# A SwiGLU block on one core: where the sums of activations are split into high and low parts, and by which engine

## The chip, the cores and the metric

The kernel runs on one core of a Trainium2 chip. The metric is the device time of one execution, in microseconds. The core has a matrix engine (TensorE, PE in the profile), three engines for elementwise work (VectorE as DVE, ScalarE as ACT, GpSimd as POOL), and SyncE (SP), which here issues most of the DMA transfers. Each engine carries out its own instructions in order; between engines there are semaphores only. SBUF is the on-chip memory from which the engines work, PSUM the banks that TensorE accumulates into.

## The reference

One decoder block: a SwiGLU feed-forward network, a mixer of three branches (RWKV-7, sparse attention, cross-attention to a memory), and a second SwiGLU network. The change touches the two SwiGLU networks alone, each of which computes, with S = 1024 tokens, D_MODEL = 1024 and D_FF = 2816:

```python
def _rmsnorm(x, g):
    xf = x.astype(jnp.float32)
    y = xf * lax.rsqrt(jnp.mean(xf * xf, axis=-1, keepdims=True) + NORM_EPS)
    return (y * g.astype(jnp.float32)).astype(x.dtype)

def _swiglu(h, w_gate, w_up, w_down):
    return (jax.nn.silu(h @ w_gate) * (h @ w_up)) @ w_down
...
x = x + 0.5 * _swiglu(_rmsnorm(x, ffn1_norm[l]), ffn1_w_gate[l], ffn1_w_up[l], ffn1_w_down[l])
...
x = x + 0.5 * _swiglu(_rmsnorm(x, ffn2_norm[l]), ffn2_w_gate[l], ffn2_w_up[l], ffn2_w_down[l])
return _rmsnorm(x, final_norm)
```

All in float32.

## The kernel before

**Numbers in two parts.** Every operand of a product is split into a high part in the type fp32r and a low part, the rest: `split` (L100 to L106) makes the high part by a copy on ACT (L103) and the low part by a subtraction on DVE or POOL (L106). `mm3` (L121 to L125) then issues three matmuls for each 128x128 block of weights: high by high (L123), high weights by low activations (L124), low weights by high activations (L125). Names in the profile: `whi` and `wlo` are the parts of weights, `wraw` weights as loaded (by SP, L110), `wS` and `ds` sums of weights, `h` and `t` the moving operands of the gates, `act` those of the down product, `rg` a tile of the ring described below.

**Gates.** The class `Gates` computes gate and up products and from them the activations. D_FF has 22 columns of 128 (f = 0 to 21). Columns 0, 1, 20 and 21 (`PLAIN`) keep their activations as they are; the other eighteen make nine pairs. In `run`, products are not computed as four blocks of a 2x2 scheme but as seven (Winograd's form): P1, P2, P6, P5, P7, P3, P4, the names of `ORDER`. One product of a pair's gate or up side is 12 matmuls of 128x128 by 128x512 that accumulate in a PSUM bank; P6 adds to P1's bank and P7 adds to P6's, so before P7 may add, an ACT copy has to take P6's value out of the bank (`copy`, L502, into a ring tile). P6, P5 and P7 follow each other.

**The sums.** `finish` gets each finished up product, multiplies it with the gate's (L387) and stores the activation to DRAM (`ad`). When the four activations a11, a12, a21, a22 of a pair are there, it forms the four sums that the down product, also in Winograd's form, needs: P5 (L401), P7 (L402), P6 (L403) and P4 (L404), one POOL subtraction after another, each into a tile of a ring of `RING` = 10 tiles. Each sum is split on the spot: a high part by ACT (L409), a low part by DVE (L410). Both parts are stored, eight stores of 256 KB per pair (L413).

**Tail.** `tail` is the down product. Its 18 middle columns go in three thirds (c = 0, 1, 2); each third has 28 products: seven groups (the names of `ORDER`) for four column pairs dp of the output, in two halves of 14 (dp 0 and 1, then 2 and 3). One product is 9 matmuls. A group is three activations of the same name; `load(g)` (L254 to L266) brings them in: the sums P5, P7, P6 and P4 come already split, by two DMAs each straight into the operand tiles (L262); the other groups come raw into one of three buffers `ar` (L265) and are split by L266, for the second of three with the low part on POOL, otherwise on DVE. The first two groups are loaded and split by `first`, while the gates end. Groups 2 to 7 are loaded as the tail begins, each later one during the second half of a third (`if dp == 3`). The weights' parts are prepared `AHEAD` = 3 products ahead. The results are added to x by DVE from PSUM (L287) or by an ACT copy to `dc` (L291) and a POOL addition (L293). Sixteen products of 12 matmuls for the plain columns end the tail.

**What sets the order.** A scheduler of the framework reorders the instructions of the program before each engine's queue is written, so an engine's order is not that of the source; the printed rows in the section on the change are from the written queues. Tiles of one tag share a fixed number of buffers, and a new tile waits for the last reader of the one whose buffer it takes.

Of the kernel before, what the change touches and what calls it, by code (L numbers as in the profile page):

```python
# [8 lines left out]
FT = mybir.dt.float32  # L9
FR = mybir.dt.float32r  # L10
AF = mybir.ActivationFunctionType
# [8 lines left out]
HALF = 512  # L20
ORDER = "P1", "P2", "P6", "P5", "P7", "P3", "P4"
PLAIN = 0, 1, 20, 21
SUMS = "P5", "P7", "P6", "P4"
NG = 8
RING = 10
AHEAD = 3
# [6 lines left out]
class Builder:  # L33
# [203 lines left out]
    def tail(self, x, wd, ad, act, xload, after, st=None):  # L237
# [3 lines left out]
        nc = self.nc  # L241
# [3 lines left out]
        pool = st.enter_context(self.tc.tile_pool(name="ffd", bufs=1, space=PSUM, reuse_waits="tile"))  # L245
# [8 lines left out]
        def load(g):  # L254

            for j, src in enumerate(groups[3 * g:3 * g + 3]):
                n = (g % NG) * 6 + 2 * j
                t = [slots[n + p][0].tile([128, HALF], FR, name=f"act{g}{j}{p}", tag=slots[n + p][1]) for p in range(2)]
                act.append(t)
                if isinstance(src, list):  # L260
                    for a, b in zip(t, src):
                        nc.sync.dma_start(a.bitcast(FT), b)  # L262
                    continue
                raw = temp("ar", HALF, 3)
                nc.sync.dma_start(raw, src)  # L265
                self.split(*t, raw, eng_lo="pool" if j == 1 else "dve")  # L266

        def blocks(c, dp):

# [34 lines left out]
        xload(0)  # L304
        xload(2)
        load(2)
        xload(1)
        xload(3)
        for g in range(3, NG):
            load(g)  # L310
        for n, (c, dp, i, g) in enumerate(ops):
# [3 lines left out]
            name = ORDER[i]  # L315
            b = banks.setdefault((c, dp), {})
# [24 lines left out]
            if dp == 3 and 3 * (g + NG) < len(groups):  # L341
                load(g + NG)
# [11 lines left out]
class Gates:  # L354
# [15 lines left out]
    def temp(self):  # L370
        return self.p.tile([128, HALF], FT, name="wS", tag="wS", bufs=3)

    def finish(self, f, half, gu, c, r=None):

        nc = self.nc
        if gu == 0:
            if r is not None:
                g = self.ring()
                nc.vector.tensor_mul(g, c, r)
                c = g  # L380
            th = self.ring()
            nc.scalar.activation(th, c, AF.Tanh, scale=0.5)
            sg = self.sg[f, half] = self.p.tile([128, HALF], FT, name="sg", tag="sg", bufs=SG)
            nc.vector.scalar_tensor_tensor(sg, th, 1.0, c, op0=OP.add, op1=OP.mult)
            return
        sg = self.sg.pop((f, half))
        nc.vector.tensor_mul(sg, sg, c)  # L387
        if r is not None:
            nc.vector.tensor_mul(sg, sg, r)
        if f in PLAIN:  # L390
            (nc.scalar if f >= 20 else nc.sync).dma_start(self.ad[f, half], sg)
            return
        pair, n = f // 2, f % 2 * 2 + half
        q = self.act.setdefault(pair, {})
        q[n] = sg
        if n != 1:
            nc.sync.dma_start(self.ad[pair, ("P1", None, "P2", "P3")[n]], sg)
        if len(q) == 4:
            a11, a12, a21, a22 = [q[j] for j in range(4)]
            t = {j: self.ring() for j in ("P5", "P7", "P6", "P4")}  # L400
            nc.gpsimd.tensor_sub(t["P5"], a12, a11)  # L401
            nc.gpsimd.tensor_sub(t["P7"], a22, a12)  # L402
            nc.gpsimd.tensor_sub(t["P6"], a22, t["P5"])  # L403
            nc.gpsimd.tensor_sub(t["P4"], a21, t["P6"])  # L404
            parts = {}
            for j in t:
                hi = self.ring().bitcast(FR)
                parts[j] = hi, t[j].bitcast(FR)
                nc.scalar.activation(hi, t[j], AF.Copy)  # L409
                nc.vector.tensor_sub(parts[j][1], t[j], hi.bitcast(FT))  # L410
            for j in t:
                for a, b in zip(self.ad[pair, j], parts[j]):
                    nc.sync.dma_start(a, b.bitcast(FT))  # L413
            del self.act[pair]

    def plain(self, fs, halves, h, r=None, loads=None, step=None):
# [973 lines left out]
class Mem:  # L1390
# [76 lines left out]
    def attend(self, m, p, po):  # L1467
# [15 lines left out]
        for j in range(4):  # L1483
# [26 lines left out]
            if late:  # L1510
                finish(*late.pop())
            late.append((j, ph, pl))
            yield
        yield
        finish(*late.pop())
        yield

# [21 lines left out]
def body(ctx, tc, A, VO):  # L1539
    nc = tc.nc  # L1540
    B = Builder(ctx, tc, A)
    drp = ctx.enter_context(tc.tile_pool(name="spill", bufs=1, space=DRAM))
# [28 lines left out]
    ad = {(f, i): drp.tile([128, HALF], FT, name=f"ah{f}{i}") for f in PLAIN for i in range(2)}  # L1571
    for p in range(1, 10):
        for n in ORDER:
            t = [drp.tile([128, HALF], FT, name=f"ad{p}{n}{j}") for j in range(2 if n in SUMS else 1)]
            ad[p, n] = t if n in SUMS else t[0]
    x2d = [drp.tile([128, S], FT, name=f"x2d{k}") for k in range(KT)]
    xnd = [drp.tile([128, HALF], FT, name=f"xnd{k}") for k in range(KT)]
    xs, ns = ExitStack(), ExitStack()
# [11 lines left out]
    with ExitStack() as fs:  # L1590
# [47 lines left out]
        with ExitStack() as st:  # L1638
            B.tail(x, A["wd1"], ad, act, lambda k: nc.sync.dma_start(x[k], A["xT"][k]),
                   finish(x, np_, nps, into(x, np_, VO["mix_norm"], h),  # L1640
                          lambda half, d: nc.sync.dma_start(x1d[d][:, halves[half]], x[d][:, halves[half]])),
                   st)
# [126 lines left out]
    with ExitStack() as fs:  # L1769
        np_, nps = B.norm_pool(fs)  # L1770
        B.more_w(fs)
        with ExitStack() as st:
# [31 lines left out]
            with tc.tile_pool(name="mgp", bufs=1, reuse_waits="tile") as mp, \  # L1804
                    tc.tile_pool(name="mgps", bufs=1, space=PSUM, reuse_waits="tile") as mps:
                raw = lambda tag: mp.tile([128, HALF], FT, name=tag, tag=tag, bufs=3)
# [122 lines left out]
```

## Time and profile before

| | us |
|---|---|
| Median of three runs | 3010.19 |
| Lowest and highest | 3002.58, 3011.4 |
| The profiled execution | 3008.93 |
| Its span | 3007.1 |

The stages of the profiled execution, cut at round moments near their borders, each with the matmuls recorded in it:

| Stage | from to (us) | length (us) | matmuls |
|---|---|---|---|
| Start and plain columns | 0 to 131 | 131.0 | 425 |
| Gates, first network (`run`) | 131 to 518.4 | 387.4 | 1495 |
| Tail, first network, and the step to the mixer | 518.4 to 763 | 244.6 | 1002 |
| Mixer | 763 to 2140 | 1377.0 | 7231 |
| Its end, and the second network's plain columns | 2140 to 2380 | 240.0 | 988 |
| Gates, second network | 2380 to 2764 | 384.0 | 1495 |
| Tail, second network | 2764 to 2990 | 226.0 | 946 |
| Final norm | 2990 to 3007 | 17.0 | 2 |

In a row of the profile that names a group, the first field is the line of the kernel, then the engine, the operation, and the tiles as output<-inputs with their sizes; behind the bar come busy time and mean length in ns, and then the time that the engine stood idle just before these instructions, with the engine and line that released it. In a row of the timeline the first two numbers are the start and the length in us, and brackets hold the idle time before it. The granted clock is the share of full speed that TensorE was allowed in that stretch.

### The profile page before, as it was taken

How to read it: one execution, taken by the hardware profiler on the slowest of the kernel's cores; microseconds unless marked ns; L12 is line 12 of the kernel's file. 1: busy time of each engine (PE TensorE's matmuls, PEld its weight loads, DVE VectorE, ACT ScalarE, POOL GpSimd, SP SyncE). 2: the span in 40 equal slices, each digit the busy share in tenths (PEclk: the TensorE clock that was granted, in tenths of full speed). 3: DMA queues.
4: the chain of work that ended last, by engine and by line, in shares of the span. 5: the costliest groups of instructions: out<-in, count | busy, mean ns of one | idle time of the engine just before them, and what ended most of it. 6: DMA issues, size and time to landing. Idle time of an engine off the chain costs nothing. (4 is left out here: it accounts for less than half of the span.)

```text
span 3007.1 us, 40911 instructions
## 1 busy us (share of the span) xinstructions
PE 2837.3 (94%) x13574; PEld 2241.2 (75%) x13574; DVE 1935.4 (64%) x3876; ACT 1373.5 (46%) x2923; POOL 1012.6 (34%) x981
## 2 busy tenths in 40 slices
PE   7899999999999999999999989999999999999997
PEld 5777777787887677776777667777787777777786
DVE  8656555767565567666565357888767466565676
ACT  5334434444454345444453356666544333334343
POOL 4434343674102011111110133333324343344672
PEclk9999999999999999999999999999999999999998
DMA  4333435754313122221222552221564333336653
GB/s 151 99 117 129 143 130 171 274 178 150 117 57 91 56 71 64 75 72 56 68 65 64 157 164 74 80 70 60 179 219 141 96 127 105 121 119 221 230 176 98
DMA packets 241520, 363.70 MB, mean 121 GB/s; under 512 B 50291, under 2 KB 90107, under 8 KB 241308
## 3 DMA queue, kind: packets, MB, share of 16 engines
q1 hardware_dynamic: 223696, 330.38, 33.8%
q10 hardware_dynamic: 17612, 30.70, 3.4%
q8 instruction: 107, 1.75, 0.2%
q14 instruction: 105, 0.86, 0.1%
HBM read 257.59 MB, written 103.40 MB: 120 GB/s over the span
## 5 line engine op out<-in xcount | busy, mean ns | idle before, releaser
L103 ACT ACTIVATE whi<-wraw 128x512 fp32r<-128x512 f32 (+1 forms) x584 | 353.2, 607 | 701.8 <-PE pgu L124 309.6
L106 DVE TENSOR_TENSOR wlo<-wraw,whi 128x512 fp32r<-128x512 f32 (+1 forms) x576 | 454.7, 794 | 303.8 <-ACT whi L103 284.7
L123 PE MATMUL mm<-h,whi 128*128 128x512 f32 x800 | 329.9, 412 | 0.2 <-ACT gbt L1662 0.2
L125 PE MATMUL mm<-h,wlo 128*128 128x512 f32 x800 | 320.8, 402 | 7.2 <-DVE wlo L106 7.2
L124 PE MATMUL mm<-h,whi 128*128 128x512 f32 x800 | 318.6, 398 | 0.0
L123 PE MATMUL pgu<-t,whi 128*128 128x512 f32 x576 | 238.0, 413 | 57.7 <-ACT rg L502 57.7
L123 PE MATMUL pgu<-h,whi 128*128 128x512 f32 x688 | 273.6, 398 | 16.8 <-ACT whi L103 15.9
L125 PE MATMUL pgu<-h,wlo 128*128 128x512 f32 x688 | 273.9, 399 | 8.0 <-DVE wlo L106 7.9
L124 PE MATMUL pgu<-h,whi 128*128 128x512 f32 x688 | 275.2, 400 | 2.2 <-DVE h L98 1.7
L123 PE MATMUL pd<-act,whi 128*128 128x512 f32 x632 | 248.7, 393 | 7.4 <-ACT whi L103 7.4
L125 PE MATMUL pd<-act,wlo 128*128 128x512 f32 x632 | 248.5, 393 | 4.5 <-DVE wlo L106 4.3
L124 PE MATMUL pd<-act,whi 128*128 128x512 f32 x632 | 247.9, 392 | 0.0
L125 PE MATMUL pgu<-t,wlo 128*128 128x512 f32 x576 | 235.4, 409 | 0.0
L124 PE MATMUL pgu<-t,whi 128*128 128x512 f32 x576 | 234.9, 408 | 0.0
L123 PEld LDWEIGHTS pgu<-t,whi 128*128 128x128 f32 x576 | 114.3, 198 | 90.5 <-ACT rg L502 66.6
L125 PEld LDWEIGHTS mm<-h,wlo 128*128 128x128 f32 x800 | 151.5, 189 | 39.9 <-DVE wlo L106 9.0
L123 PEld LDWEIGHTS mm<-h,whi 128*128 128x128 f32 x800 | 151.8, 190 | 36.4 <-issue 5.3
L124 PEld LDWEIGHTS mm<-h,whi 128*128 128x128 f32 x800 | 151.9, 190 | 28.8 <-issue 3.0
L123 PEld LDWEIGHTS pgu<-h,whi 128*128 128x128 f32 x688 | 132.8, 193 | 47.3 <-ACT whi L103 18.9
L125 PEld LDWEIGHTS pgu<-h,wlo 128*128 128x128 f32 x688 | 132.9, 193 | 40.3 <-DVE wlo L106 11.9
L124 PEld LDWEIGHTS pgu<-h,whi 128*128 128x128 f32 x688 | 133.1, 193 | 32.6 <-DVE h L98 2.7
L123 PEld LDWEIGHTS pd<-act,whi 128*128 128x128 f32 x632 | 119.8, 190 | 34.2 <-ACT whi L103 9.5
(419 smaller groups left out, 6615.6 us busy)
## 6 DMA issues: line engine op xcount, KB each, us to landing
wraw<-in_wgu SPq DMA_DIRECT2D x192, 256.0 KB, 2.7
wraw<-in_wd SPq DMA_DIRECT2D x96, 192.0 KB, 4.2
wraw<-in_win SPq DMA_DIRECT2D x52, 256.0 KB, 2.6
wraw<-in_wgb SPq DMA_DIRECT2D x48, 256.0 KB, 2.8
gd<-gbt SPq DMA_DIRECT2D x48, 256.0 KB, 2.0
gbt<-gd ACTq DMA_DIRECT2D x40, 256.0 KB, 2.9
wraw<-in_wd SPq DMA_DIRECT2D x32, 256.0 KB, 2.7
wraw<-in_wbr SPq DMA_DIRECT2D x32, 256.0 KB, 3.1
```

Source lines behind the costliest of these rows:

```text
L103: nc.scalar.activation(hi, src, AF.Copy)
L106: (nc.vector if eng_lo == "dve" else nc.gpsimd).tensor_sub(lo, src, hi.bitcast(FT))
L123: mm(ps, w[0], x[0], start=start, stop=False, **kw)
L124: mm(ps, w[0], x[1], start=False, stop=False, **kw)
L125: mm(ps, w[1], x[0], start=False, stop=stop, **kw)
```

## The change

The sums are no longer split in the gates. `finish` stores each of the four sums raw, one store of 256 KB instead of two, and P7 is written over the tile of a12 instead of into a ring tile of its own, so that a pair takes three ring tiles where it took eight, and no ACT or DVE instruction. In the tail, `load` treats every group alike: raw into one of the three buffers `ar`, the high part by ACT, the low part always by DVE, where the middle one of three was POOL's. `first` is not touched.

```diff
-SUMS = "P5", "P7", "P6", "P4"
...
                 act.append(t)
-                if isinstance(src, list):
-                    for a, b in zip(t, src):
-                        nc.sync.dma_start(a.bitcast(FT), b)
-                    continue
                 raw = temp("ar", HALF, 3)
                 nc.sync.dma_start(raw, src)
-                self.split(*t, raw, eng_lo="pool" if j == 1 else "dve")
+                self.split(*t, raw, eng_lo="dve")
...
             a11, a12, a21, a22 = [q[j] for j in range(4)]
-            t = {j: self.ring() for j in ("P5", "P7", "P6", "P4")}
+            t = {j: self.ring() for j in ("P5", "P6", "P4")}
+            t["P7"] = a12
             nc.gpsimd.tensor_sub(t["P5"], a12, a11)
             nc.gpsimd.tensor_sub(t["P7"], a22, a12)
             nc.gpsimd.tensor_sub(t["P6"], a22, t["P5"])
             nc.gpsimd.tensor_sub(t["P4"], a21, t["P6"])
-            parts = {}
             for j in t:
-                hi = self.ring().bitcast(FR)
-                parts[j] = hi, t[j].bitcast(FR)
-                nc.scalar.activation(hi, t[j], AF.Copy)
-                nc.vector.tensor_sub(parts[j][1], t[j], hi.bitcast(FT))
-            for j in t:
-                for a, b in zip(self.ad[pair, j], parts[j]):
-                    nc.sync.dma_start(a, b.bitcast(FT))
+                nc.sync.dma_start(self.ad[pair, j], t[j])
...
         for n in ORDER:
-            t = [drp.tile([128, HALF], FT, name=f"ad{p}{n}{j}") for j in range(2 if n in SUMS else 1)]
-            ad[p, n] = t if n in SUMS else t[0]
+            ad[p, n] = drp.tile([128, HALF], FT, name=f"ad{p}{n}")
```

Lines move up by up to 12 in the changed file: L409 and L410 have no counterpart, L502 is L491 there, L103 is L102, L106 is L105, L265 is L260, L382 is L377, L287 is L282.

The first place is ACT's queue in the gates, around the end of a pair. Before:

```order
L103 ACTIVATE whi<-wraw 128x512
L382 ACTIVATE rg<-rg 128x512
L103 ACTIVATE whi<-wraw 128x512 x2
L409 ACTIVATE rg<-rg 128x512 x4
L502 ACTIVATE rg<-pgu 128x512
L103 ACTIVATE whi<-wraw 128x512 x2
L502 ACTIVATE rg<-pgu 128x512
L103 ACTIVATE whi<-wS 128x512
```

The same place after:

```order
L102 ACTIVATE whi<-wraw 128x512
L377 ACTIVATE rg<-rg 128x512
L102 ACTIVATE whi<-wraw 128x512 x2
L491 ACTIVATE rg<-pgu 128x512
L102 ACTIVATE whi<-wraw 128x512 x2
L491 ACTIVATE rg<-pgu 128x512
L377 ACTIVATE rg<-rg 128x512
L102 ACTIVATE whi<-wS 128x512
```

The four copies of sums between the weights' splits and the copy out of PSUM (`rg<-pgu`) are gone, and the copy follows the splits at once.

The second place is SP's queue at the start of the first tail, where the groups 2 to 7 are loaded (`ad1P_165` and the like are the stored activations, `x` the residual rows). A piece of it before:

```order
L262 DMA act_4305<-ad1P_165 128x512
L262 DMA act_4306<-ad1P_166 128x512
L265 DMA ar<-ad1P_167 128x512
L262 DMA act_4309<-ad2P_176 128x512
L262 DMA act_4310<-ad2P_177 128x512
L262 DMA act_4313<-ad3P_187 128x512
L1639 DMA x_4260<-in_xT 128x1024
L1639 DMA x_4261<-in_xT 128x1024
L1639 DMA x_4262<-in_xT 128x1024
L1639 DMA x_4263<-in_xT 128x1024
```

And after:

```order
L260 DMA ar<-ad1P_163 128x512
L260 DMA ar<-ad2P_170 128x512
L260 DMA ar<-ad3P_177 128x512
L1627 DMA x_4071<-in_xT 128x1024
L1627 DMA x_4072<-in_xT 128x1024
L1627 DMA x_4073<-in_xT 128x1024
L1627 DMA x_4074<-in_xT 128x1024
L260 DMA ar<-ad1P_164 128x512
L260 DMA ar<-ad2P_171 128x512
L260 DMA ar<-ad3P_178 128x512
```

Loads straight into operand tiles (`act`) have become loads into `ar`, of which there are three, so that the rows behind a load that waits for a free one wait too. Further on in the same queue, after:

```order
L260 DMA ar<-ad5P_187 128x512
L1627 DMA x_4078<-in_xT 128x1024
L260 DMA ar<-ad6P_194 128x512
L109 DMA wraw<-in_wd 128x384 x6
```

The weights of the next column pairs stand behind the last load of the sixth group, where before they stood behind loads of parts.

The third place is DVE's queue in the second half of the first third, where seven groups are loaded. Before:

```order
L106 TENSOR_TENSOR wlo<-ds,whi 128x384
L106 TENSOR_TENSOR act_4678<-ar,act_4677 128x512
L106 TENSOR_TENSOR wlo<-ds,whi 128x384
L287 SCALAR_TENSOR_TENSOR x_4264<-pd,x_4264 128x512
L106 TENSOR_TENSOR act_4690<-ar,act_4689 128x512
L106 TENSOR_TENSOR wlo<-ds,whi 128x384
L287 SCALAR_TENSOR_TENSOR x_4266<-pd,x_4266 128x512
```

And after:

```order
L105 TENSOR_TENSOR act_4513<-ar,act_4512 128x512
L105 TENSOR_TENSOR act_4519<-ar,act_4518 128x512
L105 TENSOR_TENSOR wlo<-ds,whi 128x384
L105 TENSOR_TENSOR act_4525<-ar,act_4524 128x512
L282 SCALAR_TENSOR_TENSOR x_4075<-pd,x_4075 128x512
L105 TENSOR_TENSOR wlo<-ds,whi 128x384
L105 TENSOR_TENSOR act_4565<-ar,act_4564 128x512
L105 TENSOR_TENSOR act_4571<-ar,act_4570 128x512
L282 SCALAR_TENSOR_TENSOR x_4077<-pd,x_4077 128x512
L105 TENSOR_TENSOR act_4577<-ar,act_4576 128x512
```

Two subtractions of a group of three, for some of the groups, have become three for every group.

On TensorE the number of matmuls is the same, and the order differs in the gates alone: where before one to four matmuls of the next product stood ahead of P7's (the first of these is the one at 310.22 us in the prediction), now all of P6, P5, P7 and the next P1 follow each other in whole.

## The prediction

> **What bounds the kernel now.** I read the busy shares first, then the share of the clock that TensorE was granted, then the costliest groups for the idle time ahead of them.
>
> ```profile
> PE 2837.3 (94%) x13574; PEld 2241.2 (75%) x13574; DVE 1935.4 (64%) x3876; ACT 1373.5 (46%) x2923; POOL 1012.6 (34%) x981
> L123 PE MATMUL pgu<-t,whi 128*128 128x512 f32 x576 | 238.0, 413 | 57.7 <-ACT rg L502 57.7
> ```
>
> TensorE (PE) is the bound, busy 94% of the span, and the change takes no matmul away. It can therefore gain only where PE stands still or runs slowly. One group stands out: 57.7 us of PE idle ahead of matmuls on the activation sums `t`, all released by one ACT line, the copy L502.
>
> Next the stages: the gates and the down product ("tail") of the first FFN, then of the second. Columns are length, then busy time with instruction count for PE, PEld, DVE, ACT, POOL, then clock share, DMA share and GB/s.
>
> ```profile
> 131.00:518.40 387.40, 357.52 (x1495) 290.71 (x1494) 225.35 (x306) 156.24 (x267) 160.49 (x111) 0.95 0.41 136
> 518.40:763.00 244.60, 232.09 (x1002) 190.04 (x1001) 171.66 (x211) 107.26 (x204) 142.64 (x107) 0.97 0.59 203
> 2380.00:2764.00 384.00, 356.17 (x1495) 290.19 (x1494) 225.43 (x291) 149.05 (x256) 157.19 (x108) 0.96 0.38 127
> 2764.00:2990.00 226.00, 218.38 (x946) 178.47 (x945) 156.96 (x195) 94.99 (x179) 131.77 (x98) 0.98 0.54 186
> ```
>
> To price the gates I need the undisturbed spacing of matmuls, and what happens at one stall. This is PE's timeline there:
>
> ```profile
> 309.54 0.39 PE L123 MATMUL pgu<-h,whi 128*128 128x512 f32 x1
> 309.76 0.39 PE L124 MATMUL pgu<-h,whi 128*128 128x512 f32 x1
> ...
> 310.22 0.39 PE L123 MATMUL pgu<-h,whi 128*128 128x512 f32 x1
> 313.55 0.50 PE L123 MATMUL pgu<-t,whi 128*128 128x512 f32 x1 [2.95 <-ACT rg L502]
> ...
> 318.46 0.40 PE L123 MATMUL pgu<-h,whi 128*128 128x512 f32 x1
> ```
>
> Before the stall three steps take 310.22 - 309.54 = 0.68, so 0.227 us each. 1495 matmuls at 0.2267 make 338.9 us; the two gates stages last 387.4 and 384.0, so they lose 48.5 + 45.1 = **93.6 us**. The stall alone loses more than its 2.95 us of idleness, because the clock falls after it:
>
> ```profile
> 313.50:315.00 1.50, 1.45 (x6) 1.00 0.97 376
> 315.00:318.10 3.10, 3.10 (x9) 0.50 1.06 395
> 318.10:349.00 30.90, 30.90 (x137) 1.00 0.36 115
> ```
>
> The middle numbers are PE alone; the granted clock is 0.50 for 3.1 us, then 1.00 again. From 310.22 to 318.46 are 8.24 us for 15 steps (one to 313.55, and 14 more by the records) worth 3.40: **4.84 us lost at this stall**, 3.1 of them standing and 1.7 slow.
>
> Why is the copy late? ACT's and POOL's timelines at the same place:
>
> ```profile
> 307.60 0.63 ACT L409 ACTIVATE rg<-rg 128x512 fp32r<-128x512 f32 x1
> 308.85 0.64 ACT L409 ACTIVATE rg<-rg 128x512 fp32r<-128x512 f32 x1 [0.61 <-POOL rg L402]
> 310.54 0.63 ACT L409 ACTIVATE rg<-rg 128x512 fp32r<-128x512 f32 x1 [1.06 <-POOL rg L403]
> 312.39 0.63 ACT L409 ACTIVATE rg<-rg 128x512 fp32r<-128x512 f32 x1 [1.21 <-POOL rg L404]
> 312.92 0.58 ACT L502 ACTIVATE rg<-pgu 128x512 f32<-128x512 f32 x1
> ```
> ```profile
> 306.27 1.29 POOL L401 TENSOR_TENSOR rg<-sg 128x512 f32<-128x512 f32 x1 [7.45 <-DVE sg L387]
> 307.52 1.29 POOL L402 TENSOR_TENSOR rg<-sg 128x512 f32<-128x512 f32 x1
> ...
> 310.59 1.77 POOL L404 TENSOR_TENSOR rg<-sg,rg 128x512 f32<-128x512 f32 x1
> ```
>
> ACT takes its work in order. The four high parts L409 of a pair's sums stand ahead of L502, and each waits for one POOL subtraction; the last of these ends at 312.36, ACT follows at 312.39, the copy at 312.92, PE at 313.55. The copy itself was possible when P6 was done, before 307.6. There are 72 of L409, so 18 pairs:
>
> ```profile
> L409 ACT ACTIVATE rg<-rg x72: 616/630/636, 129.2 to 2731.3; 128x512 fp32r<-128x512 f32 x72
> ```
>
> 18 x 4.84 = 87 us: nearly all that the gates lose. Stalls of the same kind without any L409 ahead are two, 513.04 and its twin in the second FFN, and one at 246.64:
>
> ```profile
> 246.64 0.50 PE L123 MATMUL pgu<-t,whi 128*128 128x512 f32 x1 [1.48 <-ACT rg L502]
> 513.04 0.50 PE L123 MATMUL pgu<-t,whi 128*128 128x512 f32 x1 [0.92 <-ACT rg L502]
> ```
>
> **The change, part by part. Gates.** It removes 36 ACT copies, 36 DVE subtractions and 36 stores per FFN, and puts no wait in their place: after it, L502 stands behind splits of weights, as it does now in the products without sums. How it then goes, this stretch shows:
>
> ```profile
> 331.34 0.58 ACT L502 ACTIVATE rg<-pgu 128x512 f32<-128x512 f32 x1
> 335.98 0.39 PE L125 MATMUL pgu<-t,wlo 128*128 128x512 f32 x1
> 336.21 0.39 PE L123 MATMUL pgu<-h,whi 128*128 128x512 f32 x1
> ```
>
> P6, P5 and P7 are 36 matmuls, the last at 335.98; counted back at 0.2267, P6's last starts at 330.5 and P7's first at 333.3, with no gap. The copy is over at 331.92, 1.3 us early. So the 18 stalls and their slow patches go; the three small ones (1.48 + 2 x 0.92 = 3.3 us) stay. **Gates: 93.6 - 3.3 = 90.3 us gained**; bounds: 45 if another late operation fills half the gap, 93.6 if the small ones go too. What is late next is POOL's chain L401 to L404 itself, 6.1 us, now waited for by stores alone; a sum is needed only in the tail. P7 is written over a tile of activations and holds it for the length of its store longer than POOL's reads did, one of seven such tiles. I cost this at nothing, since DVE, which fills the next one, is busy 225 of 387 us here; if DVE did wait, it would be the second rival below. The 36 stores fewer take from a DMA share of 0.41 in this stage, where PE waits for no transfer: nothing. That the next product's first matmuls no longer stand ahead of P7 costs nothing either, PE having the same matmuls without a gap.
>
> **Tail.** Per FFN 36 loads of finished halves go, and 36 ACT copies and 36 subtractions appear here; 10 further subtractions go from POOL to DVE. ACT has room (36 x 0.63 = 23 us on 95 of 226). DVE gets 46 more, on 157 of 226. What one costs:
>
> ```profile
> L106 DVE TENSOR_TENSOR act<-ar,act x38: 678/1491/1789, 525.1 to 2924.3; 128x512 fp32r<-128x512 f32 x38
> L106 POOL TENSOR_TENSOR act<-ar,act x20: 1296/1672/1742, 534.8 to 2924.9; 128x512 fp32r<-128x512 f32 x20
> L287 DVE SCALAR_TENSOR_TENSOR x<-pd,x x128: 675/686/693, 530.4 to 2989.7; 128x512 f32<-128x512 f32 x128
> DMA to landing us min/median/max: 2.5/4.0/7.8
> ```
>
> Minimum, median and maximum in ns: a DVE subtraction from SBUF takes 0.68 alone, but 1.5 in the median; the one that reads PSUM (L287) never stretches. POOL's goes from 1.3 to 1.7. Both stretch by about the other's length, so they take turns. Alone, they follow each other at these spacings:
>
> ```profile
> 567.49 0.54 DVE L106 TENSOR_TENSOR wlo<-wraw,whi 128x384 fp32r<-128x384 f32 x1
> 567.96 0.68 DVE L287 SCALAR_TENSOR_TENSOR x<-pd,x 128x512 f32<-128x512 f32 x1
> 568.56 1.01 DVE L106 TENSOR_TENSOR wlo<-wraw,whi 128x384 fp32r<-128x384 f32 x2
> ```
> ```profile
> 557.84 1.01 POOL L279 TENSOR_TENSOR wraw<-wraw 128x384 f32<-128x384 f32 x1
> 558.81 1.33 POOL L281 TENSOR_TENSOR wraw<-wraw,ds 128x384 f32<-128x384 f32 x1
> ```
>
> That is 0.47 (384 wide) and 0.60 (512) on DVE, 0.97 and, from 306.27 and 307.52 above, 1.25 on POOL. The heaviest piece of the tail is a run of 14 products (two column pairs) in which seven groups of three activations are loaded: 126 matmuls, 28.6 us on PE. In turn-taking work it will hold, on POOL 8 x 0.97 + 6 x 1.25 = 15.3, on DVE 14 x 0.47 + 21 x 0.60 = 19.2: **34.5 us in 28.6**, 5.9 late. Up to 3 products (6.1 us) of weights are prepared ahead, which could hide all of it; bounds 0 and 5.9, I take 5.9, as DVE has eight L287 besides. There are two such runs per tail: 12 us.
>
> The tail's start is the third place. Six groups are raw now and go through three buffers `ar`; per group a transfer (2.5 to 4.0), a copy (0.63) and the subtraction (0.7 to 1.5) make 4.2 to 6.1 us, against 4.08 that PE takes for a group's two products. SP issues in order: behind a load that waits for a free `ar` stand four loads of `x`, and behind the sixth group the weights of the column pairs 2 and 3, for which ACT, DVE and at last PE wait. Behind a raw copy that waits on ACT stand copies of weights in the same way. Bounds: 0 if the slack hides it, 6 x 2 = 12 us; I take 4. Together **the tail after loses 16 us**. Before, it lost this, all near one place:
>
> ```profile
> 547.00:580.00 33.00, 31.73 (x136) 24.86 (x135) 23.84 (x25) 13.06 (x26) 22.40 (x16) 1.00 0.69 245
> 580.00:612.00 32.00, 27.24 (x108) 21.52 (x107) 20.57 (x26) 12.65 (x25) 22.20 (x18) 0.89 0.50 171
> 580.58 0.63 ACT L103 ACTIVATE act<-ar 128x512 fp32r<-128x512 f32 x1 [7.89 <-DMA ar<-ad6P]
> ```
>
> 65 us for 244 matmuls worth 55.3: 9.7, say 10. There ACT waits for a raw group queued behind twelve loads of finished halves; these loads go, so that loss goes. Net per tail 16 - 10 = +6, **both +12 us** (bounds -20 and +45).
>
> **Sum**, against the profiled execution's 3008.9 us: 3008.9 - 90.3 + 12 = 2930.6. The shown median is 1.3 above that execution: **2932 us**.
>
> **The rivals. DVE is wholly blocked (2963).** If each POOL instruction that reads SBUF stops DVE's whole queue, a heavy run costs DVE 14 x 0.47 + 29 x 0.60 + 15.3 = 39.3 us, 10.7 over. With the start, also 18 raw tiles, that is 3 x 10.7 = 32 per tail, 22 more than before: 3008.9 - 90.3 + 44 = 2963. For it speaks the median of 1.49; against it that L287 does not stretch. The Trainium skill ("SBUF — State Buffer", "Who interferes with whom") says that a DVE instruction with two SBUF inputs contends with a GpSimd one that reads SBUF, and that the later one blocks fully; the stretched rows agree, and the rule speaks for all 46 moved subtractions landing on that lock. By it the sum would be this rival's, by turn-taking with queues that fill the gaps it is mine.
>
> **Another wait takes half the gap in the gates (2976).** DVE's chain, or weights: 3008.9 - 45 + 12. For: ACT also waits for POOL's 6.1 us chain indirectly through POOL's later sums of weights. Against: the products without sums run 137 matmuls without a break (318.10 to 349.00).
>
> **Three raw buffers starve the tail (slower, about 3135).** Some 20 groups per tail go through them. A round of 4.08 us is free; if each transfer lands in 7.8 us, as the slowest did behind the x loads, a round takes 7.8 + 0.63 + 1.3 = 9.7, and 40 rounds lose 5.6 each: 3008.9 - 90.3 + 225, or 3135 to 3145 as lookahead hides some. It decides from a round of 6.6 us on, where 40 x 2.5 eats the gain and 9 us more. Against: a tail's loads of activations fall from 2 x 36 + 29 (half of the 58 raw ones in the rows above) to 65, and 2.5 us is what a quiet queue takes.
>
> **The stalls are not due to the four copies (3010).** Then removing them brings nothing. The times at 312.36 to 313.55 speak against it.
>
> **How the numbers follow.** Forecast 0.62, DVE blocked 0.20, half a gap 0.10, starved 0.05, no effect 0.03. The forecast's own range is 2908 (tail gains 10 in all) to 2948 (the heavy runs at nearly twice the cost). The range 2905 to 2968 adds the second case and leaves out the rest, 0.18. Measured differences under 0.3%, 9 us, can't be told from none: faster 0.92, same 0.03, slower 0.05.
>
> **What would show it.** Right: PE's idle time before `pgu<-t` falls from 57.7 to about 3, the gates' clock to 0.99 or 1.00, both gates stages to 340 to 343 us. The tails: 1 to 7 us longer, DVE `act<-ar` some 130 times at 1.2 to 1.5 us, ACT's wait for `ar<-ad6P` near 580 gone. Wrong: L502 still late with another instruction ahead of it on ACT; PE waiting in the tail for `wlo` of DVE (the second case) or for `act` and `wraw` with ACT idle on `ar` transfers (the fourth).

## The result, and the profile after

| | before | after |
|---|---|---|
| Median of four runs (us) | 3009.27 | 2938.71 |
| Lowest and highest (us) | 3002.58, 3011.4 | 2934.57, 2944.84 |
| The profiled execution, its span (us) | 3008.93, 3007.1 | 2934.57, 2932.8 |

The ratio is 0.9771, with a 95% interval of 0.9748 to 0.9794: faster by 2.3%. The prediction said 2932 us, range 2905 to 2968.

Where the time went, from the first to the last matmul of each stage in the two traces (gates with their plain columns: matmuls on `pgu`; tails: on `pd`):

| Stage | before (us) | after (us) | difference |
|---|---|---|---|
| Gates, first network | 511.8 | 464.2 | -47.6 |
| Tail, first network | 226.0 | 234.6 | +8.6 |
| Gates, second network | 486.5 | 442.3 | -44.2 |
| Tail, second network | 224.9 | 232.1 | +7.2 |
| The rest of the span | 1557.9 | 1559.6 | +1.7 |

So the gates gave 91.8 us, and the tails took 15.8 back. The same stages in the view by windows, after: the two `run` stretches of the gates, then the two tails (length, busy time and count of PE, PEld, DVE, ACT, POOL, clock, DMA share, GB/s).

```profile
131.00:471.00 340.00, 338.68 (x1495) 279.88 (x1495) 205.14 (x272) 136.40 (x234) 154.71 (x111) 1.00 0.38 122
2342.20:2682.40 340.20, 339.28 (x1497) 280.59 (x1496) 190.30 (x257) 129.53 (x223) 149.72 (x109) 1.00 0.35 111
471.20:706.00 234.80, 221.60 (x951) 176.40 (x949) 181.31 (x240) 117.76 (x223) 121.95 (x93) 1.00 0.52 163
2681.40:2913.80 232.40, 220.13 (x951) 176.89 (x949) 179.72 (x238) 113.97 (x212) 119.97 (x89) 1.00 0.47 146
```

The gates' 1495 matmuls now take 340.0 us where 387.4 stood, 1.1 above the undisturbed 338.9, and the granted clock there is 1.00, not 0.95. In the tails DVE is busy 181 us instead of 157. PE's idle time ahead of two groups on the page of after, and ahead of the down product's on the page of before:

```profile
L122 PE MATMUL pgu<-t,whi 128*128 128x512 f32 x576 | 224.4, 390 | 2.2 <-ACT rg L491 2.2
L124 PE MATMUL pd<-act,wlo 128*128 128x512 f32 x632 | 249.1, 394 | 20.5 <-DVE wlo L105 20.4
```
```profile
L123 PE MATMUL pd<-act,whi 128*128 128x512 f32 x632 | 248.7, 393 | 7.4 <-ACT whi L103 7.4
L125 PE MATMUL pd<-act,wlo 128*128 128x512 f32 x632 | 248.5, 393 | 4.5 <-DVE wlo L106 4.3
```

57.7 us ahead of `pgu<-t` have become 2.2; the down product, whose largest entry was 7.4, now waits 20.5 us, where it waited 4.5, for low parts of weights that DVE makes. What the gates look like at the end of a pair, ACT and then POOL:

```profile
287.79 0.63 ACT L102 ACTIVATE whi<-wraw 128x512 fp32r<-128x512 f32 x1 [1.81 <-PE pgu L123]
288.32 0.58 ACT L491 ACTIVATE rg<-pgu 128x512 f32<-128x512 f32 x1
```
```profile
287.38 1.29 POOL L397 TENSOR_TENSOR rg<-sg 128x512 f32<-128x512 f32 x1 [7.30 <-DVE sg L382]
288.75 1.62 POOL L398 TENSOR_TENSOR sg<-sg 128x512 f32<-128x512 f32 x1
290.33 1.74 POOL L399 TENSOR_TENSOR rg<-sg,rg 128x512 f32<-128x512 f32 x1
292.15 1.62 POOL L400 TENSOR_TENSOR rg<-sg,rg 128x512 f32<-128x512 f32 x1
```

POOL's chain of four is as long as ever, 287.38 to 293.77, but the copy out of PSUM is issued in its midst and waits for none of it.

Where the tails lose, read by subtracting 0.2267 us per matmul from the starts of the products (first tail, then second). Products are numbered 0 to 83; loads of groups fall into 14 to 27 and 42 to 55.

| Products | before | after |
|---|---|---|
| 0 to 13 | 0.7, 0.0 | 2.1, 0.0 |
| 14 to 27, seven groups loaded | 1.9, 1.8 | 7.1, 4.9 |
| 28 to 34, next column pairs | 7.9, 7.0 | 5.8, 5.8 |
| 35 to 55, seven groups loaded from 42 on | 0.0, 0.0 | 0.0, 0.0 |
| 56 to 62, next column pairs | 0.3, 0.0 | 4.3, 5.3 |
| 63 to 83, and the plain columns | 0.5, 1.4 | 0.5, 1.5 |
| All | 11.3, 10.2 | 19.9, 17.4 |

One piece of the new loss, products 28 to 34 of the first tail, in the timeline of after (all engines, rows of SP, ACT and PEld left out):

```profile
540.01 1.50 DVE L105 TENSOR_TENSOR act<-ar,act 128x512 fp32r<-128x512 f32 x1
540.93 1.44 POOL L270 TENSOR_TENSOR ds<-wraw 128x384 f32<-128x384 f32 x1
...
541.43 0.68 DVE L282 SCALAR_TENSOR_TENSOR x<-pd,x 128x512 f32<-128x512 f32 x1
...
542.03 0.75 DVE L105 TENSOR_TENSOR wlo<-wraw,whi 128x384 fp32r<-128x384 f32 x1
542.44 1.21 POOL L271 TENSOR_TENSOR ds<-ds,wraw 128x384 f32<-128x384 f32 x1
542.70 1.50 DVE L105 TENSOR_TENSOR act<-ar,act 128x512 fp32r<-128x512 f32 x1
...
542.84 0.50 PE L124 MATMUL pd<-act,wlo 128*128 128x512 f32 x1 [1.75 <-DVE wlo L105]
```

PE stands 1.75 us until the `wlo` of 542.03 is done. That subtraction stood in DVE's queue behind raw activations, which took 1.5 us each beside POOL's sums of weights (`ds`) for the next column pairs, as at 540.01 and 542.70. The addition from PSUM at 541.43, beside the same POOL row, took 0.68.

### The profile page after: what moved, and what is told of

It is laid out like the page before. It is cut to its first block, busy times and chain, and to the rows that moved or that the text cites. A ratio compares the mean times of both kernels' runs of the same rounds, so it can differ in the third digit from the quotient of the medians.

```text
span 2932.8 us, 40668 instructions
## 1 busy us (share of the span) xinstructions
PE 2798.3 (95%) x13574; PEld 2211.4 (75%) x13574; DVE 1921.3 (66%) x3896; ACT 1369.5 (47%) x2923; POOL 974.3 (33%) x961
## 3 DMA queue, kind: packets, MB, share of 16 engines
q8 instruction: 107, 1.75, 0.2%
## 5 line engine op out<-in xcount | busy, mean ns | idle before, releaser
L102 ACT ACTIVATE whi<-wraw 128x512 fp32r<-128x512 f32 (+1 forms) x584 | 353.0, 607 | 624.1 <-PE pgu L123 239.4
L105 DVE TENSOR_TENSOR wlo<-wraw,whi 128x512 fp32r<-128x512 f32 (+1 forms) x576 | 443.2, 773 | 296.2 <-ACT whi L102 272.6
L124 PE MATMUL pd<-act,wlo 128*128 128x512 f32 x632 | 249.1, 394 | 20.5 <-DVE wlo L105 20.4
L122 PE MATMUL pgu<-t,whi 128*128 128x512 f32 x576 | 224.4, 390 | 2.2 <-ACT rg L491 2.2
L124 PE MATMUL pgu<-t,wlo 128*128 128x512 f32 x576 | 224.1, 389 | 0.0
L123 PE MATMUL pgu<-t,whi 128*128 128x512 f32 x576 | 224.1, 389 | 0.0
L124 PEld LDWEIGHTS pd<-act,wlo 128*128 128x128 f32 x632 | 118.6, 188 | 55.5 <-DVE wlo L105 31.3
L288 POOL TENSOR_TENSOR x<-x,dc 128x512 f32<-128x512 f32 x72 | 104.4, 1456 | 136.9 <-ACT dc L286 117.9
```

The costliest lines, as they stand in the source:

```text
L102: nc.scalar.activation(hi, src, AF.Copy)
L105: (nc.vector if eng_lo == "dve" else nc.gpsimd).tensor_sub(lo, src, hi.bitcast(FT))
L122: mm(ps, w[0], x[0], start=start, stop=False, **kw)
L123: mm(ps, w[0], x[1], start=False, stop=False, **kw)
L124: mm(ps, w[1], x[0], start=False, stop=stop, **kw)
L288: nc.gpsimd.tensor_add(xd, xd, t)
```

## The experiments

All ratios are to runs of the kernel before on the same chip. "Loss" is that of the last row of the table above. Each kernel has one trace. How far a tail's length moves by itself can be read where the tail's code is that of before: 226.0, 225.0 and 226.5 us in the first network of `before`, `e1_defer` and `e7_onecopy`, but 224.9, 229.1 and 229.6 in the second. A difference of 2 to 4 us in one tail is therefore only an indication.

**The gates. The place in ACT's queue, or the work?** `e1_defer`, from the kernel before:

```diff
             nc.gpsimd.tensor_sub(t["P4"], a21, t["P6"])
+            self.later.append((pair, t))
...
+    def flush(self):
...
+            for j in t:
+                hi, lo = self.ring().bitcast(FR), t[j].bitcast(FR)
+                nc.scalar.activation(hi, t[j], AF.Copy)
+                nc.vector.tensor_sub(lo, t[j], hi.bitcast(FT))
+                for a, b in zip(self.ad[pair, j], (hi, lo)):
+                    nc.sync.dma_start(a, b.bitcast(FT))
...
                 self.finish(2 * pair + 1, 1, gu, add(copy(ps), st["z"]))
+                self.flush()
```

> The kernel before with one thing moved: the high copies, low subtractions and eight stores of a pair's sums stay in the gates, but are written out only after the next product's P7, so that ACT's copies stand behind the copy out of PSUM instead of ahead of it (P7 is written over a12, as in the change, so that ten ring tiles suffice). The tail is that of before. Theory (the place in ACT's queue is what costs): the 18 stops of 3 us and the slow clock after them go, gates 80 to 92 us shorter, tails as before (226 and 225 us), 2917 to 2930 us in all, faster than the changed kernel. Rival 1 (the work itself, 72 copies and 72 subtractions in the gates, is what costs): gates as before, 3005 to 3012. Rival 2 (another operation becomes the late one): PE waits for another line, gates 40 to 60 us shorter, 2950 to 2970.

2924.42 us, ratio 0.970 (0.9681 to 0.9719). Gates 467.9 and 443.0 us, 43.9 and 43.5 shorter; tails 225.0 and 229.1. ACT's timeline shows the four copies (L416) behind a copy out of PSUM (L507), waiting for nothing:

```profile
334.53 0.58 ACT L507 ACTIVATE rg<-pgu 128x512 f32<-128x512 f32 x1
336.45 0.63 ACT L382 ACTIVATE rg<-rg 128x512 f32<-128x512 f32 x1 [1.34 <-DVE rg L511]
336.99 1.66 ACT L416 ACTIVATE rg<-rg 128x512 fp32r<-128x512 f32 x3
338.55 0.62 ACT L416 ACTIVATE rg<-sg 128x512 fp32r<-128x512 f32 x1
```

All the work of splitting is still in the gates, and 87.4 of the 91.8 us are gained: the place in the queue was the cost, not the work. Rivals 1 and 2 of the expectation fall. (As in the change, P7 is also written over a12, and the subtractions and stores move along with the copies.)

**Stops of 3 us and the clock.** `e7_onecopy`, from the kernel before: only P4 goes through the same `flush`.

```diff
-            for j in t:
+            for j in ("P5", "P7", "P6", "P4"):
+                if j == "P4":
+                    self.later.append((pair, {j: t[j]}))
+                    continue
                 hi = self.ring().bitcast(FR)
```

> The kernel before, with only the last of the four sums, P4, split behind the next P7's copy (P7 written over a12); the other three stay ahead of the copy out of PSUM. By the timeline of before the chain of POOL's subtractions that ACT waits for ends 1.8 us earlier, so PE's stops shrink from 3.1 to about 1.3 us. Theory A (a stop of about 3 us makes the granted clock fall, a shorter one does not): the slow stretches go with 1.8 us of each stop, 18 x (1.8 + 1.75) = 64 us, gates 28 to 35 us shorter each, total 2940 to 2952. Theory B (any stop in this place is followed by slow matmuls): 18 x 1.8 = 33 us, total 2970 to 2980.

2965.27 us, ratio 0.985 (0.9827 to 0.9873): between the two. Gates 485.8 and 461.6 us, 26.0 and 24.9 shorter. PE at such a stop, then the clock behind it:

```profile
424.69 0.50 PE L123 MATMUL pgu<-t,whi 128*128 128x512 f32 x1 [1.65 <-ACT rg L518]
425.03 0.39 PE L124 MATMUL pgu<-t,whi 128*128 128x512 f32 x1
425.26 0.39 PE L125 MATMUL pgu<-t,wlo 128*128 128x512 f32 x1
```
```profile
424.60:428.00 3.40, 3.31 (x14) 1.00 0.78 302
```

The stop lasted 1.8 us by the starts (2.03 between two matmuls, less the 0.23 of one), not 1.3 as I had worked out, so the total missed both ranges; and at the 16 of 18 places where it lasted that long the matmuls behind it keep 0.23 us, as here; at the other two, of 2.0 us (136.09 and 2357.18), they took 0.43 for a while, as behind 15 of the 18 stops before the change. Shortening 18 stops by 1.3 us is 23 us, the gates gained 51: the other 28 are about what the slow stretches cost. That is theory A's mechanism with a smaller cut, as far as these single stops go; what the clock goes by is read more closely in the last section. The Trainium skill ("TensorE: Matmul & The Clock Gate", "Part 1: The HAM clock gate") ties the fall of the clock to an idle window of about 3.4 us; here stops of 3.1 us sufficed mostly, two of 2.0 us did, and none of 1.8 us. A whole idle window of that length was not needed; the measurement decides.

**The tails. The price of the splits?** `e2_nosplit`, from the kernel after:

```diff
+                if g < 21 and ORDER[g % 7] in ("P5", "P7", "P6", "P4"):
+                    for a in t:
+                        nc.sync.dma_start(a.bitcast(FT), src)
+                    continue
                 raw = temp("ar", HALF, 3)
                 nc.sync.dma_start(raw, src)
-                self.split(*t, raw, eng_lo="dve")
+                self.split(*t, raw, eng_lo="pool" if j == 1 else "dve")
```

> The changed kernel, its gates untouched; in the tail the groups of sums are loaded twice, straight into both operand tiles, with no copy and no subtraction (this leaves the splitting of the sums out), and the raw groups have the middle low part on POOL as before. Theory (the tail's +16 us is the price of 72 splits on ACT and DVE and of the passage through three buffers): tails back to 224 to 227 us, total 2917 to 2923. Rival (the tail is longer because it begins earlier or at another state of the queues, not because of the splits): tails stay at 230 to 235, total 2930 to 2940.

2924.44 us, ratio 0.970 (0.9682 to 0.9719); tails 225.8 and 225.8, loss 11.2 and 11.1 as before the change; the total is 1.4 us above its range. This kernel leaves the splitting of the sums out and has the middle low part of the other groups on POOL, as before. The additional loss is the splits' and what they pass through.

**Three buffers, or DVE?** `e3_ring5`, from the kernel after, `temp("ar", HALF, 3)` made `temp("ar", HALF, 5)`:

> The changed kernel with five raw buffers instead of three. Theory (DVE, taking turns with POOL, is what PE waits for): PE's idle time on low parts of weights stays at 15 to 25 us, tails within 4 us of 234.6 and 232.1, total 2930 to 2940. Rival (three buffers starve the splits: ACT stood 86 us waiting for raw tiles): the tails lose their 16 us or most of it, total 2917 to 2925, and ACT's waiting for raw tiles falls below 40 us.

2924.63 us, ratio 0.970 (0.9682 to 0.9719). Tails 227.5 and 227.5, loss 12.9 and 12.8. Who waited for a raw tile or its split, in after and then here (us, times):

```profile
  ACT act L102: 85.9, 68
```
```profile
  ACT act L102: 43.6, 34
```

ACT's waiting is halved and the tails give 7.1 and 4.6 us back: the three buffers held much of it. But PE's idle time on DVE barely moves, from 20.5 to this:

```profile
L124 PE MATMUL pd<-act,wlo 128*128 128x512 f32 x632 | 248.6, 393 | 17.7 <-DVE wlo L105 17.6
```

Each theory is right about its own part, and the expectation, which let one take all, was wrong for both.

**Low parts by DVE alone.** `e4_pool`, from the kernel after, with the old choice for the middle of three:

```diff
-                self.split(*t, raw, eng_lo="dve")
+                self.split(*t, raw, eng_lo="pool" if j == 1 else "dve")
```

> The changed kernel with the middle low part of each raw group on POOL, as it was before the change. Theory (DVE and POOL take turns, and a subtraction costs 1.25 us of the turn on POOL against 0.60 on DVE): the seven groups of a heavy run hold the turn 4.6 us longer, three such phases per tail, tails 5 to 14 us longer each, total 2945 to 2965. Rival (DVE's own queue is the limit, whoever holds the turn): DVE is freed of a third of its raw subtractions, tails 4 to 8 us shorter each, total 2920 to 2930.

2954.23 us, ratio 0.9804 (0.9781 to 0.9827); tails 241.9 and 242.7, 7.3 and 10.6 longer. With POOL in it, the change would have given away 18 us by the tails; the ratio is 0.003 above the change's, some 10 us, with intervals that just overlap. As a longer POOL queue also holds a raw buffer longer, `e9_pool5` is the same edit on `e3_ring5`:

> e3_ring5 (the changed kernel, five raw buffers) with the middle low part of each raw group on POOL: e4_pool without the shortage of buffers. Theory A (turns: a subtraction holds 1.25 us of them on POOL, 0.60 on DVE): tails still 4 to 12 us longer each than e3_ring5's 227.5, ratio to before 0.973 to 0.979. Theory B (e4_pool was slow because POOL's queue held one of three raw buffers too long): with five buffers the tails are 222 to 229, ratio 0.967 to 0.972.

2927.38 us, ratio 0.9722 (0.9702 to 0.9741); tails 231.1 and 230.4, 3.6 and 2.9 longer than with five buffers and DVE alone. That lies between the two expectations. The intervals of the two ratios overlap, so only the tails' lengths speak, and 3 us each is near what a tail moves by itself: at most a quarter to a half of the 7.3 and 10.6 us remains with more buffers; the rest went with the shortage of them.

**What PE waits for with five buffers: turns, or a full DVE?** `e6_dveadd`, from `e3_ring5`, replaces `copy_add` by `add`:

> e3_ring5 (the changed kernel with five raw buffers), in which the additions of P1, P6 and P7 to x are made by DVE straight from PSUM like the others, with neither ACT's copy nor POOL's addition. A run of 14 products has six of these. Theory A (what PE still waits for is the turn that DVE and POOL take: six POOL additions of 1.25 us hold it, DVE's from PSUM do not): locked work per heavy run falls from 34.5 to 27.0 us, tails 3 to 8 us shorter each, total 2908 to 2918. Theory B (with five buffers DVE's own queue is full: it was busy 18.8 of 18.8 us there): 6 x 0.60 = 3.6 us more DVE work per run, tails 4 to 12 us longer each, total 2932 to 2950.

2917.04 us, ratio 0.9702 (0.9681 to 0.9723), the same ratio as `e3_ring5`. The tails are 225.3 and 225.0, 2.2 and 2.5 shorter, though DVE has 72 additions more; PE's waiting for `wlo` falls from 17.6 to 6.4:

```profile
L124 PE MATMUL pd<-act,wlo 128*128 128x512 f32 x632 | 247.4, 392 | 6.7 <-DVE wlo L105 6.4
L122 PE MATMUL pd<-act,whi 128*128 128x512 f32 x632 | 247.6, 392 | 5.6 <-ACT whi L102 5.1
```

while 5.1 us of a new wait for ACT appear. Theory B, a full DVE, would have made the tails 4 to 12 us longer; it falls. A's 3 to 8 us shorter is missed, and as the edit takes ACT's copies away too, the shorter waiting for `wlo` isn't POOL's doing alone.

`e10_nosums`, from `e3_ring5`, leaves DVE's and ACT's list alone and takes POOL's sums of weights away:

```diff
-            s1, s2 = temp("ds", 384, 4), temp("ds", 384, 4)
-            nc.gpsimd.tensor_add(s1, a[1, 0], a[1, 1])
-            nc.gpsimd.tensor_sub(s2, s1, a[0, 0])
-            yield self.wparts(s2)
-            yield self.wparts(s1)
-            nc.gpsimd.tensor_sub(a[1, 0], a[0, 0], a[1, 0])
             yield self.wparts(a[1, 0])
-            nc.gpsimd.tensor_sub(a[0, 1], a[0, 1], s2)
+            yield self.wparts(a[1, 1])
+            yield self.wparts(a[1, 0])
             yield self.wparts(a[0, 1])
             yield self.wparts(a[1, 1])
```

> e3_ring5 with POOL's sums of weights in the tail left out (the products take the blocks themselves; this leaves part of the computation out). DVE's and ACT's instructions stay the same in number and size; POOL has eight fewer per run of 14 products. Theory A (turns): PE's idle time on the low parts of weights falls from 17.6 us to under 6, tails 3 to 8 us shorter each, DVE's subtractions of 384 columns take 0.54 to 0.65 us in the mean. Theory B (DVE's own queue is full, POOL or not): that idle time stays above 12 us, tails within 2 us of 227.5.

2900.84 us, ratio 0.9639 (0.9614 to 0.9664). Tails 217.0 and 217.9, loss 2.3 and 3.2, and

```profile
L124 PE MATMUL pd<-act,wlo 128*128 128x512 f32 x632 | 247.0, 391 | 2.1 <-DVE wlo L105 2.1
```

So DVE's list, as long as before, costs almost nothing once POOL's sums of weights are gone; theory B falls again. The subtractions of raw activations in the first tail (busy time, mean in ns), in `e3_ring5` and then here:

```profile
L105 DVE TENSOR_TENSOR act<-ar,act 128x512 fp32r<-128x512 f32 x65 | 59.1, 935 | 1.3 <-ACT act L102 1.2
```
```profile
L105 DVE TENSOR_TENSOR wlo<-wraw,whi 128x384 fp32r<-128x384 f32 x82 | 57.4, 712 | 19.2 <-ACT whi L102 19.2
L105 DVE TENSOR_TENSOR act<-ar,act 128x512 fp32r<-128x512 f32 x64 | 48.1, 777 | 4.2 <-ACT act L102 4.1
```

They fall from 0.94 to 0.78 us. Those of 384 columns fall from 0.84 to 0.71 in the mean of both tails, above the 0.65 expected. The tails are 10.5 and 9.6 us shorter, more than the 3 to 8 expected of turns: the run also removes ACT's waiting for POOL's sums, and how much is that and how much turns isn't shown.

**A kernel better than the change.** `e5_defer5` is `e1_defer` with five raw buffers:

> e1_defer (sums split in the gates, behind P7's copy) with five raw buffers instead of three. What is left of its tails' loss of 10.3 and 14.4 us lies where ACT waits 7.7 us for one raw tile whose load stands in SP's queue behind twelve loads of finished halves. Theory A (the three buffers hold these raw loads back): the loss falls to 4 to 8 us per tail, total 2908 to 2918. Theory B (it is the place in SP's queue, which more buffers do not change): tails within 2 us of 225.0 and 229.1, total 2920 to 2928.

2906.29 us, ratio 0.9668 (0.9651 to 0.9686), whose interval lies wholly below that of the change. Gates 465.8 and 442.8, tails 218.7 and 219.7, loss 4.0 and 5.0: theory A, with a total 2 us below its range. The loads of finished halves are still there, and the loss in products 28 to 34, 7.3 and 7.9 us in `e1_defer`, is down to 0.6 in both tails. PE's waits in the tail:

```profile
L125 PE MATMUL pd<-act,wlo 128*128 128x512 f32 x632 | 247.1, 391 | 2.2 <-DVE wlo L106 1.9
L123 PE MATMUL pd<-act,whi 128*128 128x512 f32 x632 | 246.6, 390 | 1.9 <-ACT whi L103 1.7
```

`e8_mix` splits P5 and P7 in the gates, P6 and P4 in the tail, again with five buffers:

```diff
-SUMS = "P5", "P7", "P6", "P4"
+SUMS = "P5", "P7"
...
+            for j in ("P6", "P4"):
+                nc.sync.dma_start(self.ad[pair, j], t[j])
+            self.later.append((pair, {j: t[j] for j in ("P5", "P7")}))
```

> Half and half: P5 and P7 split in the gates behind the next P7's copy and loaded as finished halves, P6 and P4 stored raw and split in the tail, all low parts of raw groups by DVE, five raw buffers. If the two tails' losses (ACT waiting behind loads of halves in e1_defer, DVE full in e3_ring5) each grow with the share of sums handled that way, both shrink: tails lose 4 to 9 us each instead of 10 to 14, total 2908 to 2919. If the losses have other causes than that share, tails as in e3_ring5, 2920 to 2928.

2927.04 us, ratio 0.9729 (0.9714 to 0.9744); tails 227.3 and 226.6, loss 12.6 and 12.0: as `e3_ring5`, the second expectation. Half of the tail's splits are enough to bring the loss, so between half and all it doesn't grow with the share.

## Why the prediction was right, step by step

- **The gates (90.3 us).** Measured 91.8. The cause named, four copies behind POOL's chain ahead of the copy out of PSUM, is shown by `e1_defer`, which left all of their work in place; that the slow clock goes with the stops is shown by `e7_onecopy` and by a clock of 1.00 after. The small stops, expected to stay at 3.3 us, came to 2.2 by the page.
- **The tail after (16 us each).** 19.9 and 17.4. The term was a little small, and made up wrongly. The start, charged with 4 for the three buffers, lost 2.1 and 0.0. The two heavy runs, charged with 5.9 each, lost 7.1 and 4.9 in the first and nothing in the second; what they leave behind comes due in the products after them (5.8 and 5.8, 4.3 and 5.3), where POOL makes the next column pairs' sums. I had charged the buffers to the start alone; `e3_ring5` puts them at 7.1 and 4.6 of the loss, all in the heavy runs and behind them; the start got no better. That the sum for both tails, 15.8 us against 12, came this near is in part luck: the heavy runs and the start cost less than priced, and the pieces behind the runs, put at nothing, made up for it.
- **The tail before (10 us).** 11.3 and 10.2. That this loss goes with the loads of halves was half right: the wait for `ar<-ad6P` went, but in its place, products 28 to 34, stands 5.8 us of another. And the cause given, a raw load queued behind twelve loads of finished halves, was not enough by itself: `e5_defer5` keeps these loads, and with five raw buffers in place of three the loss there goes.
- **The length of DVE's subtractions.** I expected 1.2 to 1.5 us; the median of all is now 0.69, where it was 1.49, and the mean 0.96, where it was 1.32. POOL's own low parts, which had run beside them, are gone (with them back, in `e4_pool`, the median is 1.00):

```profile
L105 DVE TENSOR_TENSOR act<-ar,act x130: 674/692/1785, 469.3 to 2850.8; 128x512 fp32r<-128x512 f32 x130
```

- **The rivals.** DVE wholly blocked was priced at 32 us per tail, which did not come; but getting in each other's way is real. In the kernel after, 69 of the 130 subtractions of raw activations overlap no POOL instruction and take 0.69 us in the mean, 0.695 at most; the 61 that overlap one take 1.28. The Trainium skill's rule ("SBUF — State Buffer", "Who interferes with whom"), by which a DVE instruction with two SBUF inputs contends with a GpSimd one that reads SBUF, agrees with these numbers; but that all the moved subtractions would land on that lock, as I had it say, did not come, since about half met no POOL instruction. Half a gap in the gates did not come. Starvation by three buffers came in a mild form, 11.7 us in all, far from the 225 of its price.

## What to carry to other kernels

Where the matrix engine waits for an engine that was long free to serve it, look at what stands ahead in that engine's queue and whom it waits for: here, writing four instructions a little later gained the gates nearly as much as taking them away, and left the work where there was room. Here a stop near 3 us mostly cost more than its length, because of the clock behind it, while single stops of 1.8 us cost their length alone; several short stops close together are no better than a long one, as the next section shows. Before work is moved to another stage, count the buffers that it will pass through there and the engines with which it will take turns.

## What the runs showed of the hardware

The length of a stop alone doesn't settle whether the clock falls: 15 of 18 stops of 3.1 us (3.3 to 3.6 between two matmuls) were followed by matmuls at 0.43 us, against two of 2.0 and none of sixteen of 1.8 us, and in the tails of the changed kernel stops of 1.9 us, and one of 2.1, were followed by none. The traces show what does. In all twelve of them the granted clock changes only at the borders of a regular grid of steps of 3.413 us, which each change meets within about 0.01 us. I added up PE's standing time within each step, from the starts of its matmuls, through both SwiGLU networks. Of 4639 steps at full clock, 4531 had less than 1.75 us of it, and none of these was followed by half the clock; 68 had more than 2.05 us, and all of them were. Of the 40 between, 16 were.

So the standing time in one step counts. The three long stops without a slow stretch were each cut by a border, into about 2.0 and 1.3, 1.8 and 1.3, 1.7 and 1.4 us. And short stops add up. In the first tail of before, no single stop takes more than 1.15 us of the step from 581.17 to 584.59, but together they take 2.62 us of it. The clock halves at the border, when the last of them has lasted 1.1 us, and stays there for two steps (PE's timeline, then length, PE's busy time and count, clock, DMA share and GB/s of the stretches):

```profile
581.67 0.50 PE L123 MATMUL pd<-act,whi 128*128 128x512 f32 x1 [1.16 <-ACT whi L103]
582.01 0.40 PE L124 MATMUL pd<-act,whi 128*128 128x512 f32 x1
583.27 0.50 PE L125 MATMUL pd<-act,wlo 128*128 128x512 f32 x1 [0.86 <-DVE wlo L106]
586.50 0.80 PE L123 MATMUL pd<-act,whi 128*128 128x512 f32 x1 [2.74 <-ACT whi L103]
```
```profile
581.17:584.59 3.42, 1.23 (x3) 1.00 1.06 397
584.59:591.41 6.82, 4.91 (x12) 0.50 0.58 215
```

DVE's subtractions with both inputs in SBUF, 0.68 us alone, were lengthened up to 1.79 us beside POOL, while its additions from PSUM stayed between 0.675 and 0.693 in the kernel before.
